# Half tiles of y shared with the scan, and the first part of the output projection begun beside the last v pieces

## The chip, the cores and the metric

The kernel runs on one core of one Trainium2 chip. TensorE (PE), VectorE (DVE), ScalarE (ACT) and GpSimd (POOL) compute; SyncE (SP) and ACT issue the transfers used here. The metric is the device time of one execution in microseconds, the median over runs.

## The reference, cut to what matters

One layer of a block with two parallel groups of heads. T = 1024 tokens, D = 1024, float32.

```
h    = rmsnorm(x)
z, xBC, dt, q, k, v = split(h @ w_in)
y_ssm = gated_norm(ssd_scan(conv(xBC), dt), z)           # (T, 1024)
y_na  = neighbourhood_attention(q, k, v, rel_pos_bias)   # (T, 1024), 16 heads
x    = x + concat([y_ssm, y_na]) @ w_out                 # contraction over 2048
x    = x + relu(rmsnorm(x) @ w_mlp_in)**2 @ w_mlp_out
```

Only the line with `w_out` is computed in another order by the change. Its contraction of 2048 is cut into four parts of 512: parts 0 and 1 take the 1024 columns of y_ssm, parts 2 and 3 those of y_na.

## The kernel before, in words

Each float32 product is made of three TensorE passes, high x high, low x high and high x low (`mm3`, lines 359 to 361). So each operand exists as a high half (`wh`, `yh`: an ACT copy that rounds) and a low half (`wl`, `yl`: the rest, from POOL or DVE).

The stages of interest lie in two planned stretches. **Plan 1** is the combined projection (tiles `pq`) with the scan beside it; it ends with eight v pieces, each a PSUM tile of 24 matmuls of 512 columns. A v piece leaves PSUM through ACT and DVE as `rb` and is stored to `v_dr` by ACT's queue. Scan results y are stored token chunk by token chunk to `y_dr`. **Plan 2** is attention, eight blocks for each of sixteen heads, with parts 0 to 2 of the output projection between its blocks. An attention block is: scores `psc` (L1393, L1394), bias and row maximum on DVE (L1397, with the bias tile `mb` made on POOL at L1328 from `braw` and `nam`), the exponential on ACT (L1409), transposes `ptp<-ident,pr` on PE (L1421), their split into `pth` (ACT, L1433) and `ptl` (DVE, L1431), and the products `pv` (L1361). Part 3 and the MLP follow.

A part n of the output projection (`w_out_part(n)`) needs four tiles of y of [128, 1024], one for each 128 columns. For parts 0 and 1 each is loaded from `y_dr` (SP, L392), turned by eight 128x128 PE transposes (`ptp<-ident,yl`, L1265) into PSUM, and split by ACT (`yh`, L1280) and DVE (`yl`, L1289); part 2 loads it turned already from `na_dr` and splits it by ACT (L1300) and POOL (L1301). Then for each of two column halves of w_out two weight tiles are loaded and split (`w_pair`: SP load of `wraw`, ACT `wh` L1227, POOL `wl` L1230), and for each of eight token tiles four products `po` of three matmuls are summed and added to x.

What sets the order: every engine issues in the program's order and an instruction that waits holds the ones behind it on its engine. The order is made ahead of time by `Plan.order`, which gives each task the earliest time that its costs allow, and takes the one that can start first, and among equals the one with the earliest due time. `Plan.follow` hands the free times of one plan to the next, but the tasks of the two plans are not mixed: all of plan 1 stands in the program ahead of all of plan 2.

Transfers take one of eight semaphore lanes in turn, in program order over SP's and ACT's queues together, and each waits for the transfer eight before it on its lane. `Plan.lanes` models that.

Of the kernel before, what the change touches and what calls it, by code (L numbers as in the profile page):

```python
# [10 lines left out]
F32 = mybir.dt.float32  # L11
F32R = mybir.dt.float32r
# [7 lines left out]
P = 128  # L20
T = 1024
# [12 lines left out]
    ("rb", 2, 1024, F32),  # L34
    ("seg", 4, 512, F32),
    ("xs", 3, 512, F32),
    ("xw", 1, 512, F32),
    ("xh", 1, 512, F32R),
    ("xl", 1, 512, F32R),
    ("sb", 1, 512, F32),  # L40
    ("bh", 1, 512, F32R),
    ("bl", 1, 512, F32R),
    ("ch", 2, 128, F32R),
    ("cl", 2, 128, F32R),
    ("st", 1, 512, F32),
    ("sh", 1, 512, F32R),
    ("sl", 1, 512, F32R),
# [3 lines left out]
    ("m", 4, 16, F32),  # L51
)


class Buffer:


    def __init__(self, tag, root=None):
        self.tag, self.root, self.tile = tag, root or self, None
        self.users, self.whole, self.made = [], [], None  # L60
# [22 lines left out]
class Plan:  # L83
# [17 lines left out]
    def part(self, b):  # L101
        return Buffer(None, b)
# [125 lines left out]
def hymba_block(  # L228
# [176 lines left out]
    def pair_loads(plan, p, after=()):  # L405
# [33 lines left out]
        for j in range(2):  # L439
# [8 lines left out]
            name="v",  # L448
        )
# [9 lines left out]

    b0s = ExitStack()  # L460
    b0 = b0s.enter_context(tc.tile_pool(name="b0", bufs=2, side="right", reuse_waits="tile"))

    with ExitStack() as ph:
# [4 lines left out]
        sp = ph.enter_context(tc.tile_pool(name="sp", bufs=1, side="right"))  # L468
# [106 lines left out]
        with ExitStack() as px:  # L575
# [174 lines left out]
        qs = p2.enter_context(tc.tile_pool(name="qs", bufs=1, side="right", reuse_waits="tile"))  # L750
        plan = Plan(
            {"mm": 3, "tp": 2, "s": 2, "v": 1, "w": 4, "raw": 4, "hl": 2, "qn": 2, "sq": 2, "rq": 2}
            | {t: n for t, n, _, _ in SCAN_TILES}
# [17 lines left out]
        for tag, n, w, d in SCAN_TILES:  # L771
            make[tag] = partial(qs.tile, [P, w], d, tag=tag, name=tag, bufs=n)

# [207 lines left out]
        st, ahead = {}, {}  # L981

        def step(n, direct, at):
# [93 lines left out]
            task("AQ", 0.42, lambda: nc.scalar.dma_start(y_dr[4 * g : 4 * g + 4, :, c, :].rearrange("f p e -> p f e"), y.t.rearrange("p (f e) -> p f e", f=4)), reads=[y], size=360, due=at + 30, name="yst")  # L1077
# [27 lines left out]
        tables()  # L1105
        first_pair = pair_loads(plan, 0, stored_halves)
# [21 lines left out]
        def run(plan, make):  # L1128
            for t in plan.order():
                for b in t.new:  # L1130
                    if b.tag in make:
                        b.t = make[b.tag]()
                with in_order():
                    t.emit()
# [32 lines left out]
    with ExitStack() as ph:  # L1167
        enter_phase(ph, 2, 2, 0)
        pa = ExitStack()
        yp, cb, yt, b1, ap = (  # L1170
# [3 lines left out]
            for n in ("yp", "cb", "yt", "b1", "ap")  # L1174
# [4 lines left out]
            | {"yl": 4, "yh": 4, "nam": 1, "braw": 1, "mb": 2, "pth": 1, "ptl": 1}  # L1179
# [10 lines left out]
        for pool_, tag, n, shape, d in (  # L1190
            (yp, "yl", 4, [P, T], F32R),
            (yp, "yh", 4, [P, T], F32R),
            (cb, "nam", 1, [P, 7 * P], F32),
            (cb, "braw", 1, [P, 384], F32),
            (cb, "mb", 2, [P, 7 * P], F32),
            (ap, "pth", 1, [P, NT, 3, P], F32R),
            (ap, "ptl", 1, [P, NT, 3, P], F32R),
            (ap, "nmx", 2, [P, 8], F32),
            (ap, "pr", 4, [P, 384], F32),
            (ap, "den", 2, [P, 2, 8], F32),  # L1200
            (yt, "yT", 2, [P, T], F32),
            (ap, "rd", 1, [16, P], F32),
            (ap, "rb", 1, [P, T], F32),
        ):
            make[tag] = partial(pool_.tile, shape, d, tag=tag, name=tag, bufs=n)
# [5 lines left out]
        sp(448, lambda: nam.t, lambda: namask_d, writes=[nam], name="nam")  # L1211
        X2 = [[Buf(None) for _ in range(2)] for _ in range(NT)]
        NA = [Buf(None) for _ in range(8)]

        def w_pair(part_, h, k2, ready=-1e3):
            raw, w = Buf("raw"), Buf("w")
            r0 = 512 * part_ + 256 * k2

            def load():
                raw.t = load_raw(  # L1220
                    w_out[0][r0 : r0 + 256, 512 * h : 512 * h + 512].rearrange("(a p) f -> p a f", p=P)
                )

            def high():
                phase["n"] += 1
                w.t = [wp.tile([P, 1024], F32R, tag=t, name=t, bufs=3) for t in ("wh", "wl")]
                nc.scalar.activation(w.t[0], raw.t, AF.Copy)  # L1227

            def low():
                nc.gpsimd.tensor_tensor(w.t[1], raw.t, w.t[0].bitcast(F32), op=sub)  # L1230

            task("SP", 0.45, load, writes=[raw], size=512, name="raw")
            task("ACT", 1.06, high, reads=[raw], writes=[w], name="wh", since=ready)
            task("POOL", 2.42, low, reads=[raw], writes=[w], name="wl")
            return w
# [8 lines left out]
        def w_out_part(n):  # L1244
            ys = []
            for f in range(4 * n, 4 * n + 4):
                yl, yh = Buf("yl"), Buf("yh")
                ys.append((yh, yl))
                if f < 8:
                    sp(  # L1250
                        512,
                        partial(lambda yl: yl.t.bitcast(F32), yl),
                        partial(lambda f: y_dr[f].rearrange("p c e -> p (c e)"), f),
                        writes=[yl],
                        name="yl",
                        late=4.0,
                    )
                    pts, sides = [], [part(yl) for _ in range(2)]
                    for h in range(2):
                        pt = Buf("tp")  # L1260

                        def turn(pt=pt, yl=yl, h=h):
                            for j in range(4):
                                c = 4 * h + j
                                nc.tensor.transpose(  # L1265
                                    pt.t[:, j * P : (j + 1) * P],
                                    yl.t.bitcast(F32)[:, c * P : (c + 1) * P],
                                    ident,
                                )

                        task("PE", 0.44, turn, reads=[sides[h]], writes=[pt], name="pty")
                        pts.append(pt)
                    for h in range(2):
                        s = slice(h * 512, (h + 1) * 512)
                        col = pcol[:, 72 + f : 73 + f]
                        a = pts[h], yh, yl, s, col
                        task(
                            "ACT",
                            0.69,
                            partial(lambda pt, yh, yl, s, col: nc.scalar.activation(yh.t[:, s], pt.t, AF.Copy, scale=col), *a),  # L1280
                            reads=[pts[h]],
                            writes=[yh],
                            name="yh",
                        )
                        task(
                            "DVE",
                            0.76,
                            partial(
                                lambda pt, yh, yl, s, col: nc.vector.scalar_tensor_tensor(  # L1289
                                    yl.t[:, s], pt.t, col, yh.t[:, s].bitcast(F32), op0=mul, op1=sub  # L1290
                                ),
                                *a,
                            ),
                            reads=[pts[h], yh],
                            writes=[sides[h]],
                            name="yl",
                        )
                else:
                    sp(512, partial(lambda yl: yl.t.bitcast(F32), yl), partial(lambda f: na_dr[f - 8], f), reads=[NA[f - 8]], writes=[yl], name="na")
                    task("ACT", 1.06, partial(lambda yh, yl: nc.scalar.activation(yh.t, yl.t.bitcast(F32), AF.Copy), yh, yl), reads=[yl], writes=[yh], name="yh")  # L1300
                    task("POOL", 2.42, partial(lambda yh, yl: nc.gpsimd.tensor_tensor(yl.t, yl.t.bitcast(F32), yh.t.bitcast(F32), op=sub), yh, yl), reads=[yh], writes=[yl], name="yl")  # L1301
            for h in range(2):
                ws = [w_pair(n, h, k2, -3.5 + 1.5 * (k2 + 2 * h) if n == 0 else -1e3) for k2 in range(2)]
                for t in range(NT):
                    pt, d = Buf("mm"), X2[t][h]
                    at = pace * (16 * n + 8 * h + t) + 6
                    for k in range(4):

                        def products(k=k, pt=pt, ws=ws, t=t):
                            yh, yl = ys[k]  # L1310
                            hi, lo = ws[k // 2].t
                            w, s = slice((k % 2) * 512, (k % 2) * 512 + 512), slice(t * P, (t + 1) * P)
                            mm3(pt.t, yh.t[:, s], yl.t[:, s], hi[:, w], lo[:, w], k == 0, k == 3)

                        task("PE", 0.682, products, reads=[*ys[k], ws[k // 2]], writes=[pt], due=at + 0.7 * k, name="po")
# [188 lines left out]
        get0_w = [w_pair(3, 0, k2) for k2 in range(2)]  # L1504
# [404 lines left out]
```

## Time and profile before

| what | value |
|---|---|
| median of 3 runs | 1619.69 us (1619.43 to 1620.1) |
| the profiled execution | 1621.97 us, of which the span is 1620.2 us |
| PE busy | 1571.8 us, 97% of the span |
| DVE, ACT, POOL busy | 1014.6, 724.0, 716.4 us (63%, 45%, 44%) |
| bytes moved | 278.73 MB, 172 GB/s over the span |
| the last matmul of plan 1 begins | 614.81 us into the span |

In the rows below, times count from the span's start. An instruction's row gives its start, its duration, engine, line, operation, output and inputs, and in brackets how long its engine stood idle before it and what released it. PEclk is the clock granted to TensorE, as a share of full speed. Matmuls overlap in the pipeline, so the distance between the starts of two rows, not the duration, is what one costs.

### The profile page before, as it was taken

Reading aid. Unit: us, or ns where it says so; the run is one execution under the profiler, and the core shown is the slowest. Engines: PE = TensorE matmul, PEld = TensorE weight load, DVE = VectorE, ACT = ScalarE, POOL = GpSimd, SP = SyncE. Lnnn points to the kernel's source line nnn. Section 1 sums busy time; section 2 is a strip of 40 time slices with the busy share of each in tenths; the row PEclk is TensorE's granted clock in tenths of the full one; section 3 lists DMA queues with packets and bytes.
Section 4 is the critical chain, followed back from the end, with each engine's and each line's share of the span. In section 5 each row is a group of like instructions: output and inputs, shape, how many; then the busy total and the mean of one; then the engine's idle time right before and its main releaser. Section 6 shows DMA issues by size and latency. Waiting matters only on the chain. (4 is left out here: it accounts for less than half of the span.)

```text
span 1620.2 us, 20741 instructions
## 1 busy us (share of the span) xinstructions
PE 1571.8 (97%) x7462; PEld 1296.2 (80%) x7462; DVE 1014.6 (63%) x1420; ACT 724.0 (45%) x1183; POOL 716.4 (44%) x520
## 2 busy tenths in 40 slices
PE   7999999999999998998999898999999989999999
PEld 5788878888888886887888786888888868888887
DVE  3777355787688834676766474543443588887763
ACT  5434333444444424665676234444444443333330
POOL 2000066774699812332254431444444464654551
PEclk9999999999999998998999999999999989999999
DMA  8112498777677688876782420544343575544332
GB/s 221 53 40 69 123 299 261 223 237 260 203 226 223 187 227 248 222 183 182 207 247 87 147 101 14 182 143 151 140 164 130 220 284 205 201 146 141 104 104 78
DMA packets 182498, 278.73 MB, mean 172 GB/s; under 512 B 14627, under 2 KB 105851, under 8 KB 182395
## 3 DMA queue, kind: packets, MB, share of 16 engines
q1 hardware_dynamic: 131595, 233.88, 47.2%
q10 hardware_dynamic: 49792, 39.85, 7.6%
q0 software_dynamic: 1008, 3.67, 0.6%
q8 instruction: 59, 0.97, 0.3%
q14 instruction: 44, 0.36, 0.1%
HBM read 191.51 MB, written 89.18 MB: 173 GB/s over the span
## 5 line engine op out<-in xcount | busy, mean ns | idle before, releaser
L365 POOL TENSOR_TENSOR wl<-wraw,wh 128x1024 fp32r<-128x1024 f32 x114 | 308.9, 2721 | 329.4 <-ACT wh L364 316.0
L364 ACT ACTIVATE wh<-wraw 128x1024 fp32r<-128x1024 f32 x126 | 132.2, 1054 | 173.8 <-PE px L1144 50.7
L359 PE MATMUL pq<-wh,hTh 128*128 128x512 f32 x512 | 204.0, 398 | 2.2 <-DVE qn L865 1.7
L360 PE MATMUL pq<-wl,hTh 128*128 128x512 f32 x512 | 200.0, 391 | 0.1
L361 PE MATMUL pq<-wh,hTl 128*128 128x512 f32 x512 | 200.1, 391 | 0.0
L1144 PE MATMUL px<-wh,ahl 128*128 128x512 f32 x512 | 162.5, 395 | 3.3 <-ACT ahl L364 3.3
L1144 PE MATMUL px<-h,wh 128*128 128x512 f32 x496 | 155.8, 394 | 1.4 <-DVE x L1590 1.4
L365 DVE TENSOR_TENSOR ahl<-ar,ahl 128x1024 fp32r<-128x1024 f32 x56 | 112.8, 2022 | 23.5 <-ACT ahl L364 22.4
L364 ACT ACTIVATE ahl<-ar 128x1024 fp32r<-128x1024 f32 x56 | 58.2, 1052 | 140.0 <-PE px L1144 74.7
L1144 PEld LDWEIGHTS px<-wh,ahl 128*128 128x128 f32 x512 | 97.1, 190 | 24.9 <-ACT ahl L364 3.7
L359 PEld LDWEIGHTS pq<-wh,hTh 128*128 128x128 f32 x512 | 96.2, 188 | 22.5 <-DVE qn L865 2.1
L361 PEld LDWEIGHTS pq<-wh,hTl 128*128 128x128 f32 x512 | 96.1, 188 | 20.7
L1144 PEld LDWEIGHTS px<-h,wh 128*128 128x128 f32 x496 | 92.7, 187 | 24.5 <-ACT h L369 1.6
L360 PEld LDWEIGHTS pq<-wl,hTh 128*128 128x128 f32 x512 | 96.3, 188 | 19.4 <-DVE wl L818 0.6
L1144 PE MATMUL px<-wl,ahl 128*128 128x512 f32 x256 | 101.0, 395 | 0.0
L1144 PE MATMUL px<-h,wl 128*128 128x512 f32 x248 | 97.7, 394 | 0.0
L1328 POOL TENSOR_TENSOR mb<-braw,nam 128x256 f32<-128x256 f32 (+1 forms) x48 | 38.5, 832 | 127.5 <-DVE nmx L1397 97.7
L1397 DVE CUSTOM_DVE_ANT_0 pr<-psc,mb 128x384 f32<-128x384 f32 (+1 forms) x128 | 65.1, 520 | 29.5 <-PE psc L1394 23.7
L1144 PE MATMUL pz<-h,wh 128*128 128x512 f32 x256 | 81.7, 399 | 0.7 <-DVE h L370 0.7
L1409 ACT ACTIVATE pr<-pr,nmx 128x384 f32<-128x384 f32 (+1 forms) x128 | 74.7, 585 | 17.2 <-DVE nmx L1397 16.5
L1431 DVE TENSOR_TENSOR ptl<-ptp,pth 128x384 fp32r<-128x384 f32 (+1 forms) x128 | 65.4, 521 | 27.0 <-ACT pth L1433 25.9
L359 PE MATMUL po<-wh,yh 128*128 128x512 f32 x192 | 81.7, 425 | 0.0
(320 smaller groups left out, 3804.3 us busy)
## 6 DMA issues: line engine op xcount, KB each, us to landing
ar<-act_dr SPq DMA_DIRECT2D x56, 512.0 KB, 4.2
act_dr<-cq SPq DMA_DIRECT2D x49, 512.0 KB, 2.7
wraw<-in_w_in_dram SPq DMA_DIRECT2D x44, 512.0 KB, 6.9
rb<-cum_dr SPq DMA_DIRECT2D x32, 512.0 KB, 6.1
wraw<-in_w_mlp_in_dram SPq DMA_DIRECT2D x32, 512.0 KB, 4.6
wraw<-in_w_mlp_out_dram SPq DMA_DIRECT2D x32, 512.0 KB, 5.4
q_dr<-hl ACTq DMA_DIRECT2D x16, 512.0 KB, 4.7
k_dr<-hl ACTq DMA_DIRECT2D x16, 512.0 KB, 3.9
```

The costliest lines, as they stand in the source:

```text
L359: nc.tensor.matmul(pt, lhsT=ah, rhs=bh, start=first, stop=False)
L360: nc.tensor.matmul(pt, lhsT=ah, rhs=bl, start=False, stop=False)
L361: return nc.tensor.matmul(pt, lhsT=al, rhs=bh, start=False, stop=last)
L364: nc.scalar.activation(hl[0], src, AF.Copy)
L365: eng.tensor_tensor(hl[1], src, hl[0].bitcast(F32), op=sub)
L1144: nc.tensor.matmul(pt, lhsT=a, rhs=b, start=f, stop=l, skip_group_check=True)
L1328: nc.gpsimd.tensor_tensor(mb.t[:, s].rearrange("p (s r c) -> p s r c", r=16, c=8), view()[:, a:b], nam.t[:, s].rearrange("p (s r c) -> p s ...
L1397: nc.vector.tensor_tensor_reduce(pr.t[:, 0:n], pt.t[:, 0:n], mb.t[:, o : o + n], scale=-1.0, scalar=3.0e38, op0=add, op1=ALU.min, accum_ou ...
L1409: nc.scalar.activation(pr.t[:, 0:n], pr.t[:, 0:n], AF.Exp, bias=nmx.t[:, b : b + 1], scale=-1.0, accum_out=den.t[:, hh, b : b + 1],)
L1431: nc.vector.tensor_tensor(lo[0], pv3, hi.bitcast(F32), op=sub)
```

## The change

Rows of y become half tiles of [128, 512], one for each half of the tokens: eight for `yh` and eight for `yl`. They are the same buffers as eleven kinds of the scan's tiles (`LENT_TILES`, sixteen tiles of 2 KB a partition), given over when the scan has used them last. The scan's `rb` gets a pool of its own.

The four y rows of part 0 are loaded, turned and split by eight `y_half` tasks inside plan 1, with due times near its end, and the two weight tiles of part 0's first column half are made there too (`first_w`). Plan 2 begins with part 0's products. Part 1 uses `y_half` for each token half; part 2 loads and splits halves. Since the products read half tiles, a half can be loaded anew once the products of its own tokens are done. The part 0 weights in plan 2 lose their times of release, and the y loads their planning allowance (`late=4.0`). `Plan.follow` caps the planned time of the transfers. Twelve more loads are issued, of half the size: 16 for 8 of y, and 8 for 4 of na.

The core of the diff:

```diff
+LENT_TILES = (
+    ("seg", 4, F32),
+    ("xs", 3, F32),
+    ("xw", 1, F32),
...
+)
...
-        self.moved, self.lanes = other.moved - zero, [at - zero for at in other.lanes]
+        self.moved = min(other.moved - zero, self.free["SP"])
+        self.lanes = [at - zero for at in other.lanes]
...
+    def y_half(plan, f, h, yh, yl, done=(), due=None):
...
+        load_task(
+            plan,
+            256,
+            lambda: yl.t.bitcast(F32),
+            lambda: y_dr[f, :, 4 * h : 4 * h + 4].rearrange("p c e -> p (c e)"),
+            reads=done,
+            writes=[yl],
+            name="yl",
+        )
...
+        def turn():
+            for j in range(4):
+                s = slice(j * P, (j + 1) * P)
+                nc.tensor.transpose(pt.t[:, s], yl.t.bitcast(F32)[:, s], ident)
...
+        task("PE", 0.44, turn, reads=[yl], writes=[pt], due=due, name="pty")
+        task("ACT", 0.69, lambda: nc.scalar.activation(yh.t, pt.t, AF.Copy, scale=col), reads=[pt], writes=[yh], name="yh")
+        task("DVE", 0.76, low, reads=[pt, yh], writes=[yl], due=None if due is None else due + 6, name="yl")
+
+    def out_weights(plan, part_, h, k2, due=None):
...
+        task("SP", 0.45, load, writes=[raw], size=512, name="raw")
+        task("ACT", 1.06, high, reads=[raw], writes=[w], name="wh")
+        task("POOL", 2.42, low, reads=[raw], writes=[w], due=due, name="wl")
...
+        for h in range(2):
+            for k in range(4):
+                y_half(plan, k, h, YT[k, h, 0], YT[k, h, 1], [YD[c, 0] for c in range(4 * h, 4 * h + 4)], when(62.0) + 4 * h + k)
+        first_w = [out_weights(plan, 0, 0, k2, when(65.0)) for k2 in range(2)]
...
         def w_out_part(n):
-            ys = []
-            for f in range(4 * n, 4 * n + 4):
...
+            for h in range(2):
+                for k in range(4):
+                    f, yh, yl = 4 * n + k, YH[k, h], YL[k, h]
+                    if n == 1:
+                        y_half(plan, f, h, yh, yl)
+                    elif n == 2:
+                        src = na_dr[f - 8, :, 512 * h : 512 * h + 512]
...
             for h in range(2):
-                ws = [w_pair(n, h, k2, -3.5 + 1.5 * (k2 + 2 * h) if n == 0 else -1e3) for k2 in range(2)]
+                ws = first_w if n == h == 0 else [out_weights(plan, n, h, k2) for k2 in range(2)]
```

SP's queue, from the loads of the first pair of heads on, before:

```order
L392 DMA kl<-k_dr 64x1024 x2
L392 DMA yl<-y_dr 128x1024 x3
L392 DMA nam<-namask_dram 128x896
L392 DMA yl<-y_dr 128x1024
L392 DMA braw<-t_dr 128x384
L319 DMA wraw<-in_w_out_dram 128x2x512 x2
L392 DMA x_5418<-in_x_dram 128x512 x3
```

The same place in SP's queue with the change; here `sz` is a load of the scan, q and k those of the first pair of heads:

```order
L395 DMA yl<-y_dr 128x512 x3
L1136 DMA sz<-sz_dr 128x512
L395 DMA yl<-y_dr 128x512 x2
L395 DMA q<-q_dr 64x1024 x2
L395 DMA k<-k_dr 64x2x1024
L395 DMA q<-q_dr 64x1024 x2
L395 DMA k<-k_dr 64x2x1024
L498 DMA wraw<-in_w_out_dram 128x2x512
L395 DMA kl<-k_dr 64x1024
L395 DMA yl<-y_dr 128x512
L498 DMA wraw<-in_w_out_dram 128x2x512
```

The loads of y and of the first two weight tiles moved from behind the loads of q, k and kl to among and ahead of them, and two halves of y (not shown) stand ahead of these rows.

ACT's queue from the last v piece's copy out of PSUM on, before (`pr` is the exponential of an attention block):

```order
L855 ACTIVATE rb<-pq,rcol 128x8x64
L857 DMA v_dr<-rb 128x1024
L1280 ACTIVATE yh<-ptp,pcol 128x512 x2
L1227 ACTIVATE wh<-wraw 128x1024
L1409 ACTIVATE pr,den<-pr,nmx 128x256
L1227 ACTIVATE wh<-wraw 128x1024
L1409 ACTIVATE pr,den<-pr,nmx 128x384
L1280 ACTIVATE yh<-ptp,pcol 128x512
L1433 ACTIVATE pth<-ptp 128x2x128
```

With the change, begun one v piece earlier (its second `rb` is the last v piece's):

```order
L919 ACTIVATE rb<-pq,rcol 128x8x64
L487 ACTIVATE yh<-ptq,pcol 128x512
L505 ACTIVATE wh<-wraw 128x1024
L487 ACTIVATE yh<-ptq,pcol 128x512
L505 ACTIVATE wh<-wraw 128x1024
L487 ACTIVATE yh<-ptq,pcol 128x512
L921 DMA v_dr<-rb 128x1024
L919 ACTIVATE rb<-pq,rcol 128x8x64
L921 DMA v_dr<-rb 128x1024
L505 ACTIVATE wh<-wraw 128x1024
L1416 ACTIVATE pr,den<-pr,nmx 128x256
L1416 ACTIVATE pr,den<-pr,nmx 128x384 x2
```

Two `wh` and all `yh` of part 0 moved ahead of the last two `v_dr` stores and so of the exponentials; a third `wh`, for the second column half, now stands right ahead of the first exponential.

PE's rows from the end of the last v piece (`pq`) on, before:

```order
L361 MATMUL pq<-wh,hTl 128x512
L1393 MATMUL psc<-k,q 128x256
L1394 MATMUL psc<-kl,q 128x256
L1393 MATMUL psc<-k,q 128x384
L1394 MATMUL psc<-kl,q 128x384
L1265 MATMUL ptp<-ident,yl 128x128 x8
L1393 MATMUL psc<-k,q 128x384
L1394 MATMUL psc<-kl,q 128x384
L1393 MATMUL psc<-k,q 128x384
L1394 MATMUL psc<-kl,q 128x384
L1421 MATMUL ptp<-ident,pr 128x128 x2
L1265 MATMUL ptp<-ident,yl 128x128 x4
```

With the change the first two blocks' scores are followed by seven products `po` of part 0, whose last three rows and what stands behind them are:

```order
L364 MATMUL po<-wh,yl 128x512
L1400 MATMUL psc<-k,q 128x384
L1401 MATMUL psc<-kl,q 128x384
L1400 MATMUL psc<-k,q 128x384
L1401 MATMUL psc<-kl,q 128x384
L362 MATMUL po<-wh,yh 128x512
L363 MATMUL po<-wl,yh 128x512
L364 MATMUL po<-wh,yl 128x512
L1428 MATMUL ptp<-ident,pr 128x128 x5
L1400 MATMUL psc<-k,q 128x384
L1401 MATMUL psc<-kl,q 128x384
```

The transposes of y are gone from here; they stand, four at a time, between the matmuls of the last v pieces.

PE's rows at the transposes of part 1's y, before:

```order
L1393 MATMUL psc<-k,q 128x256
L1394 MATMUL psc<-kl,q 128x256
L1265 MATMUL ptp<-ident,yl 128x128 x16
L1421 MATMUL ptp<-ident,pr 128x128 x3
L1265 MATMUL ptp<-ident,yl 128x128 x4
L1393 MATMUL psc<-k,q 128x384
L1394 MATMUL psc<-kl,q 128x384
L359 MATMUL po<-wh,yh 128x512
```

With the change:

```order
L481 MATMUL ptp<-ident,yl 128x128 x4
L1400 MATMUL psc<-k,q 128x384
L1401 MATMUL psc<-kl,q 128x384
L1400 MATMUL psc<-k,q 128x384
L1401 MATMUL psc<-kl,q 128x384
L1428 MATMUL ptp<-ident,pr 128x128 x3
L1368 MATMUL pv<-pth,v 128x384
L1368 MATMUL pv<-ptl,v 128x384
L1400 MATMUL psc<-k,q 128x256
L1401 MATMUL psc<-kl,q 128x256
L481 MATMUL ptp<-ident,yl 128x128 x4
```

The sixteen transposes in a row became four groups of four with blocks' work between them, and those of the second token half stand over a hundred rows later.

More of the change, by code (lines that the diff above doesn't have):

```diff
@@ L448, in pair_loads @@
             name="v",
+            **free,
         )
@@ L749, in hymba_block @@
         p2 = ExitStack()
-        qs = p2.enter_context(tc.tile_pool(name="qs", bufs=1, side="right", reuse_waits="tile"))
+        yp = pa.enter_context(tc.tile_pool(name="yp", bufs=1, side="right", reuse_waits="tile"))
+        qs, qr = (
+            p2.enter_context(tc.tile_pool(name=n, bufs=1, side="right", reuse_waits="tile"))
+            for n in ("qs", "qr")
+        )
         plan = Plan(
             {"mm": 3, "tp": 2, "s": 2, "v": 1, "w": 4, "raw": 4, "hl": 2, "qn": 2, "sq": 2, "rq": 2}
-            | {t: n for t, n, _, _ in SCAN_TILES}
+            | {t[0]: t[1] for t in SCAN_TILES + LENT_TILES}
+            | {"rb": 2}
             | {"q0": 1, "k0": 1, "kl0": 1, "v0": 1}
@@ L772, in hymba_block @@
             make[tag] = partial(qs.tile, [P, w], d, tag=tag, name=tag, bufs=n)
+        make["rb"] = partial(qr.tile, [P, T], F32, tag="rb", name="rb", bufs=2)
+        for tag, n, d in LENT_TILES:
+            make[tag] = partial(yp.tile, [P, 512], d, tag=tag, name=tag, bufs=n)
         make |= tiles_of_pair(0, b0)
@@ L981, in hymba_block @@
         st, ahead = {}, {}
+        YD = {cg: Buf(None) for cg in steps}
         def step(n, direct, at):
@@ L1173, in hymba_block @@
             )
[L1174 removed]
+            for n in ("cb", "yt", "b1", "ap")
         )
@@ L1178, in hymba_block @@
             {"mm": 2, "tp": 2, "s": 2, "v": 2, "w": 3, "raw": 2}
-            | {"yl": 4, "yh": 4, "nam": 1, "braw": 1, "mb": 2, "pth": 1, "ptl": 1}
+            | {"nam": 1, "braw": 1, "mb": 2, "pth": 1, "ptl": 1}
             | {"nmx": 2, "pr": 4, "den": 2, "yT": 2, "rd": 1, "rb": 1}
@@ L1211, in hymba_block @@
         sp(448, lambda: nam.t, lambda: namask_d, writes=[nam], name="nam")
+        YH, YL = ({(k, h): Buf(None) for k in range(4) for h in range(2)} for _ in range(2))
+        for (k, h, w), b in YT.items():
+            (YH, YL)[w][k, h].t = b.t
+        first_w = [plan.given(Buf("w"), w.t) for w in first_w]
         X2 = [[Buf(None) for _ in range(2)] for _ in range(NT)]
         NA = [Buf(None) for _ in range(8)]
[L1215 to L1235, printed above, removed]
         def halves_of(yh, yl, src, lo):
@@ L1244, in w_out_part @@
         def w_out_part(n):
-            ys = []
-            for f in range(4 * n, 4 * n + 4):
[L1247 to L1301, printed above, removed]
@@ L1503, in hymba_block @@
                 w_out_part(2)
-        get0_w = [w_pair(3, 0, k2) for k2 in range(2)]
+        get0_w = [out_weights(plan, 3, 0, k2) for k2 in range(2)]
         plan.follow(before)
```

70 lines of the change are left out of this document (46 added, 24 removed).

## The prediction

> **What bounds the kernel now.** The page's first part comes first: it shows whether one engine is the bound.
>
> ```profile
> PE 1571.8 (97%) x7462; PEld 1296.2 (80%) x7462; DVE 1014.6 (63%) x1420; ACT 724.0 (45%) x1183; POOL 716.4 (44%) x520
> ```
>
> PE is the bound, and the change removes no matmul. So it can only win PE's idle time and the time in which PE runs at a low clock. The second view cuts the stretches around the change at the points where the granted clock changes. Its columns are length, PE busy time (instructions), PEclk, DMA share and GB/s.
>
> ```profile
> core 0: us, PE busy (x), PEclk, DMA share, GB/s
> 615.03:620.30 5.27, 2.29 (x16) 1.00 0.55 201
> 620.30:623.70 3.40, 3.27 (x13) 0.50 0.64 193
> 623.70:627.10 3.40, 0.61 (x2) 1.00 1.03 302
> 627.10:633.95 6.85, 5.80 (x21) 0.50 1.04 220
> 633.95:651.00 17.05, 15.02 (x91) 1.00 1.06 314
> 651.00:654.45 3.45, 3.45 (x12) 0.51 1.05 252
> 654.45:660.00 5.55, 5.55 (x37) 1.00 0.70 255
> 726.00:732.90 6.90, 5.43 (x27) 1.00 1.03 247
> 732.90:746.55 13.65, 10.76 (x37) 0.50 1.00 342
> 840.00:850.00 10.00, 8.26 (x45) 1.00 0.99 370
> ```
>
> Work at clock 0.50 takes twice its time, so half of its busy time is lost. Spot 1, the seam of the plans (615.03 to 660): of 44.97 us PE is busy 35.99, so 8.98 idle; at half clock it is busy 3.27 + 5.80 + 3.45 = 12.52, of which 6.26 lost; 15.2 together. Spot 2, the start of part 1 (726 to 746.55): idle 1.47 + 2.89 = 4.36 and 10.76 / 2 = 5.38; 9.7. Spot 3, the start of part 2: 1.7 idle. In all 26.7 us are to be had.
>
> The waits of PE (in all, times, longest), asked for spot 1, spot 2 and spot 3 in turn, name what they wait for:
>
> ```profile
> PE ptp L1265 <- DVE yl L1289: 3.8, 2, 3.1
> PE psc L1393 <- DVE nmx L1397: 3.0, 1, 3.0
> PE ptp L1421 <- DVE ptl L1431: 2.0, 1, 2.0
> ...
> PE ptp L1265 <- DMA yl<-y_dr: 2.4, 2, 2.2
> ...
> PE po L361 <- POOL yl L1301: 1.5, 2, 0.9
> ```
>
> The engine named last is seldom the cause. Behind it stand loads, as SP's waits (580 to 645), its timeline and ACT's show:
>
> ```profile
> SPq L392 <- DMA v_dr<-rb: 17.9, 4, 5.1
> SPq L319 <- DMA v_dr<-rb: 8.3, 2, 4.9
> ...
> 561.87 1.13 SPq L392 DMA_DIRECT2D q<-q_dr  x2
> ...
> 605.45 0.32 SPq L392 DMA_DIRECT2D yl<-y_dr  x1
> 614.68 5.63 SPq L319 DMA_DIRECT2D wraw<-in_w_out_dram  x2
> ...
> 624.28 1.06 ACT L1227 ACTIVATE wh<-wraw 128x1024 fp32r<-128x1024 f32 x1 [4.06 <-DMA wraw<-in_w_out_dram]
> 647.70 1.06 ACT L1227 ACTIVATE wh<-wraw 128x1024 fp32r<-128x1024 f32 x1 [3.18 <-DMA wraw<-in_w_out_dram]
> ```
>
> SP waits 26.2 us in six places for v_dr stores: by the lanes each load of plan 2 waits for a store of a v piece. So the second weight load issues near 620, ACT stands 4.06 us at its `wh`, and the first exponentials, the y splits and PE stand behind.
>
> **The change part by part.** The prices, single instructions and loads (median to landing last):
>
> ```profile
> 561.67 0.60 PE L869 MATMUL ptq<-ident,qn 128*128 128x128 f32 x4
> 562.03 0.48 PE L359 MATMUL pq<-wh,hTh 128*128 128x512 f32 x1
> 636.36 0.39 PE L359 MATMUL po<-wh,yh 128*128 128x512 f32 x1
> 636.59 0.39 PE L360 MATMUL po<-wl,yh 128*128 128x512 f32 x1
> L1280 ACT ACTIVATE yh<-ptp,pcol 128x512 fp32r<-128x512 f32 x16 | 10.9, 686 | 13.3 <-PE ptp L1265 12.1 <-DVE rb L856 1.2
> L1289 DVE SCALAR_TENSOR_TENSOR yl<-ptp,pcol,yh 128x512 fp32r<-128x512 f32 x16 | 11.9, 750 | 20.0 <-ACT yh L1280 19.9
> L1230 POOL TENSOR_TENSOR wl<-wraw,wh 128x1024 fp32r<-128x1024 f32 x14 | 33.5, 2396 | 40.4 <-ACT wh L1227 40.3
> 617.24 2.37 POOL L1328 TENSOR_TENSOR mb<-braw,nam 128x384 f32<-128x384 f32 x3
> L1471 POOL TENSOR_TENSOR yT<-yT,rb 128x512 f32<-128x512 f32 x16 | 20.5, 1308 | 7.9 <-DMA rb<-rd_dr 7.9
> L1409 ACT ACTIVATE pr<-pr,nmx 128x384 f32<-128x384 f32 x96 | 58.6, 611 | 12.9 <-DVE nmx L1397 12.7
> L1433 ACT ACTIVATE pth<-ptp 128x384 fp32r<-128x384 f32 x96 | 46.3, 489 | 34.6 <-PE ptp L1421 33.9
> wraw<-in_w_out_dram SPq DMA_DIRECT2D x16, 512.0 KB, 6.0
> sz<-sz_dr SPq DMA_DIRECT2D x16, 256.0 KB, 3.2
> yl<-y_dr SPq DMA_DIRECT2D x8, 512.0 KB, 10.7
> ```
>
> *Loads of y and first weights in plan 1.* They stand among the q and k loads, which SP issued from 561.87. Even at 10.7 us the y halves land before about 577. PE reaches the first four transposes some 45 v matmuls before plan 1's end, at 0.23 each about 605. So 28 us of cover; cost nothing. If it were gone, PE would stop in mid v piece. SP's part is eight half loads and two weight loads; the last scan load `sz` is moved behind five of them, 1.6 us at 0.32 each. I cost that at nothing, since PE's waits have no row at all between 545 and 615; its bound is 1.6.
>
> *Transposes of part 0.* Eight groups of four, 562.03 − 561.67 = 0.36 us each, 2.9 us, move into the v pieces; plan 1's PE work ends near 617.9. Each needs the PSUM tile of the group two before it, free after 0.69 (ACT) and 0.75 (DVE). Groups stand three or six matmuls apart, two groups 2.1 us or more: no wait. These 2.9 us are paid before too, partly at half clock, so they add nothing.
>
> *The seam with the change.* Count from the v pieces' end. POOL makes the two `wl` one after the other (2.40 each), the first once ACT has copied a weight tile in the last piece: they end near −1.2 and +1.2, and `mb` (2.4 for a head's three pieces) at 3.6. PE has scores of two blocks (0.6) and seven products of 0.69, until 5.4, and needs the second `wl` at 2.0 only. DVE's first row maximum comes near 3.5, with `mb`'s second piece. Two more scores and one product carry PE to 6.8, where it wants the first exponential. That stands on ACT behind the third `wh`, whose load goes out when the first `wl` has read its tile, at −1.1. With the 6.0 us median it lands at 4.9, `wh` ends at 6.0, the first two exponentials at 6.5 and 7.2: about 0.5 us of idle PE. Where it lands sooner, none; as late as the 10.7 of y's loads, 4.5.
>
> Then six blocks run with no product of part 0 between them. ACT has 0.61 + 0.49 + some 0.1 for each, 7.2; PE some 5: 2 us idle. No row of before shows such a stretch. Its bounds are nothing, as in the stretch 654.45:660.00, and 4, as in the 633.95:651.00 and 651.00:654.45 rows (2.03 idle and 1.7 lost to the clock). I keep 2.5 for the stretch, between them since the gaps would be spread, and 3.0 for the seam.
>
> On the clock, the row first: one wait of 2.0 us (`ptl`, above) was enough for the half clock from 651.00. The Trainium skill's page "TensorE: Matmul & The Clock Gate" (HAM oscillation) states the rule as no idle gaps above some 3.4 us, on a free-running window of 3413 ns. By the rule alone the idle left at the seam costs idle only, and the sum is 0.5 better; the row says a gap of 2 may cost 1.7 more. The trace's half-clock stretches do last one, two or four such windows (3.4, 6.85, 13.65).
>
> *Part 1 by halves.* A y half of the first tokens can be loaded when part 0's products of those tokens are done, four token tiles (27 us at the planned pace of 6.8) before part 1 begins; before, the whole rows were loaded only after the last, and PE waited 2.2 us for them. Transposes come in four groups with blocks between, so the chain PE, ACT, DVE (0.36 + 0.69 + 0.75 = 1.8) lies beside work. I keep 1.5 of the 9.7, between nothing and 4.4 (the idle stays, the clock does not fall).
>
> *Part 2 by halves.* POOL makes 1.31 (L1471's shape) eight times for 2.4 four times, 0.9 us more in all, ACT 0.8 more; both have slack. The first products need halves only. I keep 1.0 of 1.7.
>
> *Twelve more loads* of 256 KB cost SP 12 x 0.33 = 4 us over some 300; each lands in 3.2 (sz). The Trainium skill's page "DMA: Bandwidth & Descriptors" (Rules for kernel authors) speaks against them: one large transfer rather than several small ones. No row here shows y in halves; at 10.7 us each, as the whole rows took, they would still be hidden by the 27 us above.
>
> The sum: 15.2 − 3.0 = 12.2, 9.7 − 1.5 = 8.2, 1.7 − 1.0 = 0.7; 21.1 us. The profiled execution took 1621.97 (span 1620.2 and 1.8 around it), so it would take 1600.9. The median of the runs, 1619.69, is 2.3 lower: 1598.6. The order of loads after part 2 shifts by a few rows; 1.5 either way.
>
> **The rivals.**
> *The third weight load becomes the wait.* If it lands like the y loads (10.7; the DMA share was 1.03 to 1.06 there), ACT holds all exponentials: 4.5 idle and half a window or two of clock, 1.7 to 3.4, some 6.5 more than I keep: 1605. For it: rows 624.28 and 647.70 are this very wait. Against: y, `nam`, `braw` and two weights no longer load there.
> *Part 1 keeps its stall.* If its loads still meet the q, k and w_out loads of 720 to 740 (share 1.03), only the chain is shortened: half of the 8.2 stays, 1602.7; with some of the first rival, 1606.
> *Slower.* The y halves sit in lanes behind v_dr stores after all, as plan 2's loads do in the SP rows. The eighth then issues near 620 and lands 3.2 to 10.7 later; PE, which has it in the middle of a v piece at about 613, stops 10 to 18 us, then for the weights (4 to 6), and runs on at half clock (3.4): 18 to 27 lost, I take 24, 1623. It decides against the change when the last y half lands after some 626. Against it: in the order these loads stand ahead of the v stores.
> *No change.* The clock falls anyway in the blocks without products and in part 1, and everything but some 3 us is given back: 1618.
>
> **How the numbers follow.** My forecast 0.60, the third weight load 0.17, part 1 keeps its stall 0.11, no change 0.05, slower 0.07. Below lies the full 26.7 and 1.5 of the order: 1591.5. Above, the first two rivals reach 1606, and both with a seam at its bound of 4 some 1611; leaving out the last two cases, 0.12. Range 1592 to 1611. A measurement tells 0.2%, 3.2 us: faster 0.88, within 0.05, slower 0.07.
>
> **What would show it.** Right: PE full to the end of the v pieces, which come 2.9 us later; no half clock in the 30 us behind; the wait at part 1 for y's load gone; part 2's wait under 1 us. Wrong: a wait of ACT's `wh` for `wraw` over 3 us near 621; PE waiting for y in a v piece; half clock near 625 or 735.

## The result

Six runs each on the same chip: the kernel with the change takes 1603.32 us (median, 1599.98 to 1611.29), the kernel before 1619.43 (1618.43 to 1620.1). The ratio is 0.9908 with the interval [0.9885, 0.9931]: 16.1 us less, some five less than the 21.1 forecast. The profiled execution took 1602.66 us with a span of 1600.9, 19.3 us below the span before.

The first part of its page, PE's row:

```profile
PE 1560.6 (97%) x7462; PEld 1290.7 (81%) x7462; DVE 1016.3 (63%) x1420; ACT 722.1 (45%) x1187; POOL 717.1 (45%) x524
```

The matmuls are as many as before. PE's busy time fell from 1571.8 to 1560.6, so 11.2 us of the 19.3 is busy time, most of it work that no longer runs at half clock (the mean granted clock rose from 0.986 to 0.992, which comes to some 9.5 us); the other 8.1 is idle time (1620.2 − 1571.8 = 48.4 against 1600.9 − 1560.6 = 40.3).

The stretches of the profile with the change (length, PE busy time, PEclk, DMA share, GB/s), from the last v piece to the start of part 2:

```profile
core 0: us, PE busy (x), PEclk, DMA share, GB/s
610.00:620.00 10.00, 10.00 (x55) 1.00 0.31 100
620.00:630.00 10.00, 9.98 (x58) 1.00 0.94 270
630.00:640.00 10.00, 10.00 (x62) 1.00 1.06 224
640.00:650.00 10.00, 8.76 (x55) 1.00 1.07 244
650.00:660.00 10.00, 10.00 (x60) 1.00 1.05 209
695.00:705.00 10.00, 7.13 (x36) 0.88 1.01 322
705.00:720.00 15.00, 15.00 (x79) 0.85 0.67 162
720.00:730.00 10.00, 9.05 (x61) 1.00 1.06 334
730.00:746.55 16.55, 16.55 (x100) 1.00 0.57 156
840.00:850.00 10.00, 10.00 (x60) 1.00 0.65 207
```

Spot 1, the seam, lost 15.2 us before and loses 1.3 now, with no half clock. Spot 2 loses 1.0 of 9.7. Spot 3 loses nothing. The rows 695.00:705.00 and 705.00:720.00 are new: idle time and half clock stand where before lost nothing at all between 660 and 710:

```profile
660.00:710.00 50.00, 50.00 (x300) 1.00 0.82 206
```

PE's waits for the seam (600 to 660), for 660 to 715, and for 715 to 765 (in all, times, longest):

```profile
PE pv L1368 <- DMA q<-q_dr: 1.2, 1, 1.2
...
PE pv L1368 <- DVE yT L1389: 2.9, 1, 2.9
...
PE ptp L1428 <- ACT yh L487: 0.9, 1, 0.9
```

Each stretch has one wait. The middle one is the new loss. Its chain in the timeline (start, duration, and in brackets the idle time before it and what ended that):

```profile
661.39 0.26 ACT L1463 COPY rd<-ptp 16x128 f32<-16x128 f32 x1 [0.71 <-PE ptp L1462]
...
670.92 0.33 SPq L395 DMA_DIRECT2D rd_dr<-rd  x1
...
684.63 2.42 POOL L1335 TENSOR_TENSOR mb<-braw,nam 128x384 f32<-128x384 f32 x3 [7.16 <-DMA braw<-t_dr]
...
691.95 0.32 SPq L395 DMA_DIRECT2D na_dr<-yT  x1
...
701.58 0.58 ACT L1388 COPY yT<-pv 64x512 f32<-64x512 f32 x1 [5.04 <-DMA na_dr<-yT]
...
703.02 0.55 PE L1368 MATMUL pv<-pth,v 128*128 128x256 f32 x1 [2.87 <-DVE yT L1389]
```

`yT`, the turned output of a pair of heads, has two buffers. ACT's copy for the third pair must wait until the first pair's `yT` has been stored to `na_dr`, and everything behind it on ACT waits too. SP issued that store at 691.95. Before the change it issued at almost the same time, although the first copy into `yT` then came 11.8 us later (642.4 against 630.6):

```profile
694.43 0.52 SPq L392 DMA_DIRECT2D na_dr<-yT  x1
```

So attention got ahead and the store did not. The store itself went out as soon as POOL had scaled `yT` (689.35 to 691.92); the time was lost ahead of that. The scale `rd` was ready at 661.65, but SP, whose queue is in program order, sent it to `rd_dr` only at 670.92: loads of q, kl, x and a bias stood ahead of it, and then SP waited 5.3 us for a load of v, the transfer eight before it. Before, `rd` was ready at 676.42 and went out at 676.45. Then POOL stood 7.16 us for another bias load, and `mb` and a `wl` stood ahead of the scaling in its order. The transfers from 630 on are full: the DMA share is 1.06, 1.07 and 1.05 in the rows above, and 1.03 from 660 to 690, where before had 0.78.

### The profile page after: what moved, and what is told of

Its sections match the earlier page's. It is cut to its first block, busy times and chain, and to the rows that moved or that the text cites. A ratio compares the mean times of both kernels' runs of the same rounds, so it can differ in the third digit from the quotient of the medians.

```text
span 1600.9 us, 20796 instructions
## 1 busy us (share of the span) xinstructions
PE 1560.6 (97%) x7462; PEld 1290.7 (81%) x7462; DVE 1016.3 (63%) x1420; ACT 722.1 (45%) x1187; POOL 717.1 (45%) x524
## 5 line engine op out<-in xcount | busy, mean ns | idle before, releaser
L1219 PE MATMUL pz<-wh,ahl 128*128 128x512 f32 x256 | 80.7, 391 | 0.8 <-DVE ahl L368 0.8
```

Of the source, the lines that this page charges most:

```text
L1219: nc.tensor.matmul(pt, lhsT=a, rhs=b, start=f, stop=l, skip_group_check=True)
```

## The experiments

All ratios are against the kernel before on the same chip, where its medians were 1619.4 to 1622.2. Unless another base is named, an edit is one to the kernel with the change. The table gives what PE lost in the profiled execution, idle time and the part lost to the clock together, summed over windows of 5 us; it is one execution each, and two of the same kernel differ by up to 3.4 us in a column (the first two rows with the change).

| kernel | median us | ratio, interval | 600–665 | 665–715 | 715–765 | 765–860 | 860–1010 |
|---|---|---|---|---|---|---|---|
| before | 1619.43 | | 14.5 | 0.0 | 9.9 | 1.9 | 11.8 |
| the change | 1603.32 | 0.9908 [0.9885, 0.9931] | 1.3 | 5.6 | 1.0 | 0 | 12.6 |
| e1, the change again | 1606.3 | 0.9896 [0.9876, 0.9917] | 4.7 | 4.7 | 1.0 | 0 | 11.0 |
| e2, third `yT` | 1598.81 | 0.9857 [0.9837, 0.9878] | 3.3 | 0.0 | 0.5 | 0 | 13.7 |
| e3, no loads of x | 1600.26 | 0.9869 [0.9848, 0.9889] | 1.7 | 0.1 | 0.4 | 0 | 12.9 |
| e4, weights in plan 2 | 1607.22 | 0.9917 [0.9895, 0.9938] | 2.3 | 8.6 | 0.7 | 0 | 19.5 |
| e5, y in plan 2 | 1606.36 | 0.9913 [0.9899, 0.9926] | 5.4 | 6.3 | 0.7 | 0 | 14.9 |
| e6, part 1's y loads late | 1607.78 | 0.9921 [0.9908, 0.9934] | 4.3 | 2.0 | 4.8 | 0 | 12.7 |
| e7, x added later | 1621.62 | 1.0006 [0.9992, 1.002] | 4.8 | 0 | 3.5 | 13.5 | 16.1 |
| e9, neither in plan 1 | 1606.51 | 0.9915 [0.9897, 0.9933] | 5.2 | 0.2 | 1.5 | 0 | 11.2 |
| e10, before with `rb` apart | 1616.31 | 0.9978 [0.9964, 0.9991] | 9.4 | 0 | 9.6 | 2.0 | 10.0 |
| e11, `rb` in the old pool | 1605.43 | 0.9905 [0.9885, 0.9925] | 7.4 | 3.1 | 1.0 | 0 | 11.2 |
| e12, e9 with third `yT` | 1607.6 | 0.9917 [0.9898, 0.9936] | 4.1 | 7.8 | 1.0 | 0 | 17.9 |
| e13, e2 with x first | 1603.92 | 0.9893 [0.9876, 0.9911] | 0.0 | 8.2 | 0.5 | 0 | 13.1 |

### What holds PE at 703

**e1** is the kernel with the change once more, beside the others.

> The changed kernel once more, unedited, to see where its executions differ (1599.98 to 1611.29 us in six, against 1618.43 to 1620.1 before). Theory A (the stores of na_dr come late behind full transfers, between 690 and 705): its new profile shows PE idle and a low clock again within 20 us of 703, by another amount than 2.87 and 5.2 us, and elsewhere the same as in the first profile within 1 us. Theory B (the spread lies in the MLP or at the start, not in the attention): 690 to 720 as in the first profile within 0.5 us, and the difference of the span shows after 900.

PE's waits from 600 to 765:

```profile
PE pv L1368 <- DVE yT L1389: 3.6, 1, 3.6
PE pv L1368 <- DVE ptl L1438: 3.0, 1, 3.0
PE ptp L1428 <- ACT yh L487: 0.9, 1, 0.9
```

The wait for `yT` is there again, as Theory A has it. But the rest is not the same within 1 us: the seam loses 3.4 more, nearly all of the 3.8 by which this span is longer (1604.7 against 1600.9). The second wait is the seam's: in this execution DVE stood still at 647 for a load of x, a residual tile to which part 0 is added, and `ptl` stood behind it:

```profile
647.21 0.69 DVE L1326 TENSOR_TENSOR x<-x,po 128x512 f32<-128x512 f32 x1 [4.82 <-DMA x<-in_x_dram]
```

**e2** gives `yT` a third buffer, so that the third pair's copy does not need the first pair's store.

```diff
-            | {"nmx": 2, "pr": 4, "den": 2, "yT": 2, "rd": 1, "rb": 1}
+            | {"nmx": 2, "pr": 4, "den": 2, "yT": 3, "rd": 1, "rb": 1}
...
-            (yt, "yT", 2, [P, T], F32),
+            (yt, "yT", 3, [P, T], F32),
```

> A third buffer for yT, so that ACT's copy of the third pair need not wait for the first pair's store to na_dr. Theory A (two buffers of yT and a late store make the stall near 703): the stall goes, 5 us less, 1597 to 1599, and the executions lie within 4 us of each other. Theory C (the transfers themselves are the bound from 630 to 705, with their share over 1.0): the stall turns into a wait for loads of q, k, v or the next na rows of about the same size, and the time stays at 1601 to 1605 with the same spread.

It took 1598.81 (1597.11 to 1599.11), the fastest of all kernels here, 7.5 below e1 in the medians; the two intervals barely touch. The stretches 660 to 690 and 690 to 710, and the store's issue on SP:

```profile
660.00:690.00 30.00, 30.00 (x181) 1.00 0.97 243
690.00:710.00 20.00, 20.00 (x124) 1.00 0.91 260
```

```profile
694.72 0.33 SPq L395 DMA_DIRECT2D na_dr<-yT  x1
```

The store is as late as ever, and PE is full: what cost the time was the buffer that waited for it. The seam's wait (2.0 for `ptl`) stays.

**e3** leaves out part 0's sixteen loads of x, and DVE copies the products where it added them to x; its output lacks x.

```diff
+                    add_in = lambda v, pt: nc.vector.tensor_tensor(v, v, pt.t, op=add)
                     if n == 0:
-                        sp(256, ..., writes=[d], name="x", since=0.5)
+                        add_in = lambda v, pt: nc.vector.tensor_copy(v, pt.t)
```

> The sixteen loads of x in part 0 are left out and the first sums are copied instead of added, so the output lacks x: 4 MB of the 23 MB that SP loads from 620 to 720 are gone, and sixteen places in the lanes. Theory C (full transfers): the wait near 703 goes though yT has two buffers, DMA share falls under 0.95 there, 1595 to 1599, spread under 4 us. Theory A in its narrow form (only the order of the store): the store stays as late and the stall of 3 us with half clock stays, 1600 to 1604.

It took 1600.26. With 4 MB less to move, SP sends `rd` at 660.90, as soon as it is ready, and issues the store 11 us earlier. With two buffers there is no wait at 703, and the DMA share is 0.81 from 660 to 690:

```profile
680.92 0.33 SPq L395 DMA_DIRECT2D na_dr<-yT  x1
```

So two edits that have nothing in common but this chain both remove the loss. That the store is late because of the loads ahead of its chain is shown by e3. Whether it is their bytes or their sixteen places in SP's queue and in the lanes is not: e3 takes away both.

**e7** keeps the loads of x but moves them behind the start of part 1 into two tiles of their own, from which POOL adds them.

```diff
+                    if n == 0:
+                        xr = Buf("xr")
+                        sp(256, ..., writes=[xr], name="x", since=at + 110)
+                        task("POOL", 1.2, ..., reads=[xr], writes=[d], due=at + 140, name="xr")
```

> Nothing left out: the loads of x move behind the start of part 1, into two tiles of their own, and POOL adds them (16 x 1.2 us on POOL); part 0's first sums are copied. yT keeps two buffers. Theory C (the x loads fill the transfers from 620 to 700 and DVE waits 4.8 us for one of them at 647): the wait near 645 and the one near 703 both go, the store to na_dr issues near 680 instead of 692 to 696, 1595 to 1599, spread under 4 us. Theory A (the buffer of yT alone): the wait near 703 stays over 2 us, 1600 to 1605.

It took 1621.62, no better than before and far from the 1595 to 1599 expected. The store goes out at 683.02 and nothing is lost at 665 to 715, as in e3. But the seam keeps its wait (3.3, behind a bias load for which POOL stood 12.96 us until 647.59), and 13.5 are lost from 765 on. DVE's waits from 765 to 860 and PE's longest from 715 on:

```profile
DVE x L1325 <- POOL x L1332: 6.1, 3, 2.8
```

```profile
PE po L362 <- DVE x L1325: 6.9, 5, 2.8
```

POOL's additions are late, DVE's for the next part wait for them, and PE's products wait for the PSUM tiles that DVE holds. The load on the transfers was traded for a chain over three engines.

**e13** has e2's third `yT` and issues half of part 0's x loads ahead of the second pair's q and k, against the wait at 647.

```diff
-        free = dict(since=4.0) if p == 1 else {}
+        free = dict(since=12.0) if p == 1 else {}
```

> The changed kernel with three yT, and the loads of the second pair of heads released by the planner at 12 us instead of 4, so that eight loads of x stand ahead of them. Theory X (what is left at the seam is DVE waiting 3.8 us near 646 for a load of x that stands behind the pair's): that wait falls under 1 us, the 2 to 3 us lost from 640 to 660 go, 1594 to 1598. Rival (the transfers are full, whoever is first the other is late): PE or DVE waits as long for k, q or v of the second pair near 650, 1597 to 1602.

It took 1603.92. The seam's wait is gone, and a longer one has taken its place, at 677:

```profile
677.52 0.90 PE L1428 MATMUL ptp<-ident,pr 128*128 128x128 f32 x3 [5.99 <-DVE ptl L1438]
...
675.44 1.06 ACT L505 ACTIVATE wh<-wraw 128x1024 fp32r<-128x1024 f32 x1 [7.90 <-DMA wraw<-in_w_out_dram]
```

Behind it stands a weight load, not the q, k or v that the rival named. It took 11.7 us from its issue at 663.73 to ACT's start on it, 7.0 in e2 (675.16 to 682.18); the DMA share from 660 to 690 is 1.04, 0.97 in e2. But ACT's copy of it also stands three exponentials earlier in its order than in e2. So the wait moved and did not go; whether the full transfers or the new order moved it is not separated.

### What won the seam

**e4** makes part 0's first weights in plan 2 again, with y still ahead; **e5** does the reverse; **e9** leaves both in plan 2, so that only the half tiles, `rb`'s pool and the freed planning times remain.

```diff
# e4
-        first_w = [out_weights(plan, 0, 0, k2, when(65.0)) for k2 in range(2)]
...
-                ws = first_w if n == h == 0 else [out_weights(plan, n, h, k2) for k2 in range(2)]
+                ws = [out_weights(plan, n, h, k2) for k2 in range(2)]
# e5 (the half tiles are then taken at plan 2's start)
-                y_half(plan, k, h, YT[k, h, 0], YT[k, h, 1], ...)
...
-                    if n == 1:
+                    if n < 2:
                         y_half(plan, f, h, yh, yl)
# e9: both
```

> Part 0's first two weight tiles are made in plan 2 again, y stays in plan 1. By the prediction's own steps POOL then makes both wl only after the last v piece, 2.4 us each: PE waits for the first near 5 us behind the v pieces, 4 to 6 us idle and one or two windows of half clock at 620 to 640, 1606 to 1612. Rival (the y rows alone were the gain, the weights hide behind attention blocks that the planner puts there instead): the seam keeps under 2 us of idle time and the time stays within 2 us of the changed kernel.

> The first weights stay in plan 1, the loads, transposes and splits of part 0's y go back to plan 2, as half tiles. Theory Y (the seam waited for y): the loads stand behind plan 1's transfers in the lanes again, PE has no products until a load, a transpose, ACT and DVE are through: 8 to 13 us lost from 615 to 660, 1609 to 1616. Rival W (the seam waited for the weights, as the 4.06 us wait of ACT's wh suggests): under 4 us lost there, within 3 us of the changed kernel's 1603 to 1606.

> Neither y nor weights of part 0 in plan 1; the half tiles and parts 1 and 2 by token halves stay. With the kernels that have one of the two this makes a square. Theory Y: as with y alone in plan 2, within 3 us, since with y ahead the weights cost nothing (2.3 us idle at the seam). Rival W: the weights are worth 5 us more where y is late too. By both, 730 to 750 keeps under 2 us lost, so that 1608 to 1613 is left against 1619 to 1624 before.

They took 1607.22, 1606.36 and 1606.51, all within a microsecond of e1's 1606.3 and some 14 below before (1 − 0.9915 of some 1621). PE's waits from 600 to 665 and its longest from 665 to 765, of e4:

```profile
PE psc L1398 <- DVE nmx L1402: 2.3, 3, 1.3
...
PE ptp L1426 <- ACT pr L1414: 6.6, 1, 6.6
```

of e5:

```profile
PE psc L1395 <- DVE nmx L1399: 3.4, 1, 3.4
...
PE ptp L1423 <- ACT pr L1411: 4.0, 1, 4.0
```

and of e9 from 600 to 665:

```profile
PE psc L1393 <- DVE nmx L1397: 2.8, 4, 1.3
```

With nothing made ahead the seam loses 5.2, not 15. In e4 the seam loses 2.3, no more than in the two executions with the change: at the seam the weights made ahead show no gain. The 6.6 of e4 is the chain of `yT` again, as ACT's waits say:

```profile
ACT yT L1386 <- DMA na_dr<-yT: 7.9, 1, 7.9
```

In e5 ACT's longest wait there is for weights (`wh` for `wraw`, 5.3). What the seam gains by making y ahead, some 3 us (5.2 against 2.3, no more than two executions of one kernel differ by), is lost again behind it, where e9 loses 0.2.

So what took 9 us from the seam in e9? SP's rows of e9:

```profile
581.53 0.34 SPq L395 DMA_DIRECT2D nam<-namask_dram  x1
581.98 0.70 SPq L395 DMA_DIRECT2D braw<-t_dr  x1
582.77 1.86 SPq L498 DMA_DIRECT2D wraw<-in_w_out_dram  x2
592.70 3.23 SPq L395 DMA_DIRECT2D yl<-y_dr  x4
```

Before, `nam` went out at 600.13 and the two weights at 614.68. Two things differ. The weights stand ahead of the loads of y in e9's queue, behind them before. And the lanes differ: those loads of before waited 26.2 us in six places for `v_dr` stores, and in e9 SP's waits name no `v_dr` store at all.

**e10** puts the lanes by themselves into the kernel before: only `rb` gets its own pool. The order of each engine's instructions up to the end of attention is unchanged; the lanes, and with them the waits, are not.

```diff
-    ("rb", 2, 1024, F32),
...
-        qs = p2.enter_context(tc.tile_pool(name="qs", bufs=1, side="right", reuse_waits="tile"))
+        qs, qr = (
+            p2.enter_context(tc.tile_pool(name=n, bufs=1, side="right", reuse_waits="tile"))
+            for n in ("qs", "qr")
+        )
...
+        make["rb"] = partial(qr.tile, [P, T], F32, tag="rb", name="rb", bufs=2)
```

**e11** takes that pool away from the kernel with the change (`rb` back in `qs`).

> The kernel before with one edit: the scan's rb, which the v pieces use to their end, in a pool of its own behind the other scan tiles. Each engine's order of work in both plans is that of before; only the places of plan 2's first eight loads in the lanes move, from behind the last v store to among the v stores. Theory L (the seam's stall is those lanes): the loads issue between 581 and 600, ACT's wh no longer waits 4.06 us, 6 to 12 of the seam's 15.2 us go, 1608 to 1613 where before has 1620, with part 1's stall of 9 us still there. Rival H (half rows and planning, not lanes, made the seam short in the kernel with neither part ahead): under 3 us less than before.

> The changed kernel with rb back in the scan's other pool: y and first weights stay in plan 1, but nam, braw and all that follows take their lanes behind the last v store again. Theory L: nam and the head's bias come late, DVE has no bias tile for the first blocks, 3 to 6 us more are lost from 615 to 660 than in the changed kernel, 1606 to 1612. Rival P (having y and weights ready covers the seam by itself): the seven products and what follows hide it, within 2 us of the changed kernel's 1603 to 1606.

SP's rows of e10:

```profile
576.15 8.49 SPq L391 DMA_DIRECT2D yl<-y_dr  x3
585.86 0.33 SPq L391 DMA_DIRECT2D nam<-namask_dram  x1
...
593.08 1.24 SPq L318 DMA_DIRECT2D wraw<-in_w_out_dram  x2
```

The weights go out 21.6 us earlier with no other edit, and the seam loses 9.4 where it lost 14.5. SP still waits 10.0 us for `v_dr` stores, in two places. ACT's wait of 4.06 at 624 is gone, but one of 4.69 for a later weight load stands at 643. The time is 1616.31, a ratio of 0.9978 [0.9964, 0.9991]: some 3.6 us, real but below the 6 to 12 expected of it. From here to e9, with halves and planning but nothing made ahead, it is 9.8 us in the medians, to which part 1's stretch gives most (9.6 lost in e10, 1.5 in e9).

In e11 `nam` goes out only at 622.56, and PE waits for a row maximum that needs it:

```profile
622.56 0.33 SPq L395 DMA_DIRECT2D nam<-namask_dram  x1
```

```profile
PE psc L1397 <- DVE nmx L1401: 5.6, 1, 5.6
```

The seam loses 7.4, but the stretch after it 1.6 less than in e1, and the time is the same (1605.43). So without the pool the rest of the change still takes 7 of the 14.5 from the seam: the two cover each other in part.

By the profiled executions the seam's 13 us divide about so: the lanes 5 (before to e10), half tiles and planning 4 (e10 to e9), y ahead 3 (e9 to e4), weights ahead none to be seen. Each is a difference of single executions with an uncertainty of some 3 us, so only the first two together, 9, are sure. The shares hold for this order of edits alone, as e11 shows, and no run has y and weights ahead without the halves and the planning.

**e12** asks whether making ahead is worth something once the wait at 703 is gone: e9 with e2's third `yT`.

> Y and weights of part 0 in plan 2, half tiles, rb in its own pool, and a third buffer of yT. If the wait near 703 was that buffer alone, and the lanes were the seam, then this comes within 3 us of the changed kernel with three yT (1598.8): 1598 to 1603, executions within 4 us. If putting y ahead into plan 1 has a worth of its own it shows here: 3 to 6 us slower than 1598.8.

It took 1607.6, 8.8 more than e2, and the intervals are apart. So beside a third `yT` making ahead has a worth, more than the 3 to 6 that the expectation gave it, though beside two none could be told in the time. That worth is not at the seam: e12's seam loses 4.1, e2's 3.3. The difference lies at 665 to 715 (7.8 against 0.0) and at 860 to 1010 (17.9 against 13.7), in the slowest of e12's six executions. PE's wait in the first, and POOL's longest behind it:

```profile
PE po L363 <- POOL wl L508: 4.8, 1, 4.8
```

```profile
POOL mb L1328 <- DMA braw<-t_dr: 16.6, 1, 16.6
```

A bias load is late, POOL stands 16.6 us before it, until 675.84, makes `mb` and then the weights, and PE has waited for these until 680.55. The DMA share from 660 to 690 is 1.04: another late load under full transfers, with another victim.

### Part 1

**e6** keeps the halves but lets part 1's loads of y wait for part 0's last product.

```diff
+        part0 = Buf(None)
...
-                        y_half(plan, f, h, yh, yl)
+                        y_half(plan, f, h, yh, yl, [part0])
```

> Part 1's loads of y halves wait for the last product of part 0, as whole rows had to. The prediction's step (early loads take away the wait): PE waits for a load again near 725, 2 us or more, and a low clock follows: 4 to 9 us lost between 715 and 745, 1606 to 1613. Rival (splitting the sixteen transposes into groups between blocks is enough, the load is not what counted): under 2 us lost there and the changed kernel's time within 2 us.

It took 1607.78. PE's waits from 715 to 765:

```profile
PE ptp L481 <- DMA yl<-y_dr: 1.8, 1, 1.8
PE psc L1401 <- DVE nmx L1405: 1.5, 2, 0.9
```

The wait for y is back (the first half is issued at 718.49, 692.49 in the change), and the stretch loses 4.8. So of the 8.9 us won at spot 2, the early loads carry about 4 (4.8 to 1.0). The other 5 (9.9 to 4.8) fit the chain cut into halves, but no run undoes that by itself. In time e6 can't be told from e1: their intervals overlap.

## Why the prediction was right, and where not

The time is inside the range and the sign is right. By the prediction's own steps:

- *The v pieces end 2.9 us later, with no wait.* Right: the last matmul of plan 1 begins at 617.78 (614.81 before, 2.97 later), and PE is full from 610 to 640. The last y half is issued at 567.48 and PE has no wait between 545 and 620, so the rival *slower* is out.
- *The third weight load.* It issued and landed as forecast or sooner. The timeline of the change:

```profile
616.76 2.74 SPq L498 DMA_DIRECT2D wraw<-in_w_out_dram  x2
...
621.01 1.06 ACT L505 ACTIVATE wh<-wraw 128x1024 fp32r<-128x1024 f32 x1 [2.12 <-DMA wraw<-in_w_out_dram]
```

  Forecast were an issue 1.1 us before the v pieces' end (616.9) and a landing 4.9 behind it (622.9); it landed by 621.01, ACT waited 2.12 and PE not at all. The first rival, with over 3 us here, is out.
- *Six blocks without products.* They cost nothing (10.00 of 10.00 from 630 to 640). The seam's loss is late loads at 645 to 649 instead: for q in one execution (1.2), for x in e1 (3.0). The 3.0 kept for the seam lies between the 1.3 and the 4.7 measured, but for another cause than argued.
- *Part 1 by halves.* 1.0 lost where 1.5 was kept; the second rival is out. The early loads carry about 4 of it, as e6 shows; that the shorter chain carries the rest is argued.
- *Part 2 by halves.* Nothing lost where 1.0 was kept: 1.0 better.
- *What the prediction missed.* No step asked what is late next behind the seam. Attention runs 11.8 us earlier there against stores and loads that do not, and 5.6 us are lost at 703 for a buffer of `yT`. With it the sum would have been 15.5 plus what the three spots did better: 24.0 us won at the three spots (13.2, 8.9, 1.9), less 5.6 here and 1.6 in small changes elsewhere, is 16.8 in the losses added up; the span shows 19.3, and the 2.5 between them is not placed (the clocks added up are rounded to 0.01).
- *The cause of the seam's gain.* Here the argument failed although the sum held. The prediction read rightly that plan 2's loads stood in lanes behind `v_dr` stores, and took the cure to be that y and the first weights are issued ahead of them. e9 and e10 show that some 9 of the 13 come without that: by the line it had no term for, `rb`'s own pool, which shifts the lanes, and by the halves and planning with it. In e9, with neither made ahead, the time is that of the change. That the seam's term came out so near is in this respect luck. What making ahead does by itself stays open: e11 wins 7 at the seam without the pool, and e12 shows a worth of 8.8 us further on, once `yT` has three buffers.
- *A slip in a rival.* For *no change*, some 3 us below 1619.69 is 1616.7, not 1618. Nothing else rests on it.

A gap under 3.4 us can bring the half clock, as the row of before had it and the rule cited beside it did not: the Trainium skill's page "TensorE: Matmul & The Clock Gate" (HAM oscillation) puts the harmful gap above some 3.4 us, while a gap of 2.87 at 703 brought the clock of the change down, and 3.01 at 649 that of e1 (stretches of the change and of e1):

```profile
700.00:710.00 10.00, 7.13 (x24) 0.66 0.68 225
```

```profile
650.00:660.00 10.00, 10.00 (x51) 0.83 1.04 207
```

7.13 x 0.34 = 2.4 us of clock beside 2.87 of idle time. The gap of 1.24 at 646 cost none. The length alone does not decide it, though: in e6 a gap of 1.83 at 727 was followed by half clock and one of 1.86 at 706 was not, and in e10 one of 3.53 left the clock at 1.00 from 646 to 655:

```profile
645.93 0.30 PE L1425 MATMUL ptp<-ident,pr 128*128 128x128 f32 x1 [3.53 <-DVE ptl L1435]
```

What else decides it, no run shows.

Not settled: why executions spread as they do. Those with the change spread over 11 us where before spread over 2 on the same chip, but on the chips of the experiments 11 to 17 executions of before spread over 7 to 10. e2's four spread over 2.0, but so do e6's (2.6) and e5's (2.9) with two `yT`, so the wait for `yT` does not explain it. e4, e5, e7 and e12 lose 2 to 7 us more than the change at 860 to 1010, in one execution each, and no run asked why.

## What to carry to other kernels

When a stall is removed, ask what the work behind it will now meet earlier than before, above all buffers that are freed by a store: here one more buffer of `yT` was worth 7.5 us (e1 to e2), and the change with that third buffer is the fastest version measured. Where transfers take semaphore lanes in program order, an edit that changes no engine's order can still move loads by 20 us, so read the queue's own waits in the trace before crediting the edit that looks responsible. And undo the parts one at a time: the sum of this prediction was good while its largest term was mostly won by parts that it had not credited. Ask it again in the faster kernel, too: beside two `yT` no worth of making ahead could be told in the time, beside three it was 8.8 us.

## What had not been expected of the hardware

- Between 630 and 690 the transfers are full (DMA share 1.03 to 1.07). In e13, with loads of x moved forward there, the wait of 2.0 at the seam (e2) became one of 6.0 at 677: it moved and did not go.
- No cost of the twelve more and smaller loads was seen: e9, which has the halves, loses 0.2 at 665 to 715 and 1.5 at 715 to 765, where the whole rows lost 9.9. No run has the halves alone.
- A gap's length does not tell whether the half clock follows: 2.0 us at the seam was enough in e2 (the 3.3 lost there are the 2.0 and 1.3 of clock), 1.83 in e6, while 3.53 in e10 cost no clock.
